# Keys, queries and convolution states turned by VectorE's 32x32 blocks, gates one block later, the ending's mean and root per 128 tokens

## The chip, the cores and the metric

The kernel runs on one core of one Trainium2 chip. The metric is the device time of one execution in microseconds (us). A core has TensorE (PE, matmuls), VectorE (DVE), ScalarE (ACT), GpSimd (Pool) and a queue engine (SP), each with a program of its own that it goes through in order; they wait for each other through semaphores.

## The reference

One layer of a decoder is computed for 256 new tokens (prompt) and 8 running sequences of 4 tokens (sample), 288 tokens in all, with a model width of 2048, all in float32. Cut to its core:

```python
proj = x @ w_in
gB, gC, h, q, k, v, z, b_logit, a_logit, m_a, m_b = split(proj)
conv_out, new_conv_a = causal_depthwise_conv(gC * h, conv_a_buf, conv_a_w)      # width 3
y_a = (gB * conv_out) @ w_a_out
qkv, new_gdn_buf = causal_depthwise_conv(concat([q, k, v]), gdn_buf, gdn_conv_w) # width 4
q, k, v = split(silu(qkv))
qh, kh, vh = l2norm(q), l2norm(k), v                      # 8 heads of 128
beta = sigmoid(b_logit)
g = -exp(a_log) * softplus(a_logit + dt_bias)
o, S = gated_delta_rule(qh, kh, vh, g, beta, S0)          # chunks of 64 tokens
o = o * rsqrt(mean(o * o) + eps) * gdn_norm_w * silu(z)
y_b = o @ w_b_out
merged = sigmoid(m_a) * y_a + sigmoid(m_b) * y_b
x = layer_norm(ALPHA * x + merged @ w_o, ln1)
x = layer_norm(ALPHA * x + square(relu(x @ w_up)) @ w_down, ln2)
```

Outputs are y for prompt and sample, the last rows of both convolutions (2 rows of 1024 and 3 rows of 3072 per sequence), and the delta-rule states S.

## The kernel before

Channels lie on the 128 partitions and the 288 tokens along the free dimension. The weights are read from DRAM once, in 496 blocks of 128 x 4 x 256 values (512 KB). For each block, ACT writes a rounded copy, `hi` (`split_hi`, line 187), and DVE the remainder, `lo` (`split_lo`, recorded at its helper's line 142); PE multiplies the high and low halves of the activations with `hi` (line 217) and the high half with `lo` (line 219), 24 products per block. `raw`, `hi` and `lo` have four buffers each, so the split of block n waits until PE is done with block n-4.

The main loop goes over the blocks. Iteration i issues, in this order: the hi of block i+3, one step of the side work (from block 8 on), the lo of block i+3, the evacuations that are due, the matmuls of block i, and the load of block i+7. What is issued in one iteration runs on each engine in program order; so a product of the side work stands on PE between two blocks, and PE stands still if its operand is late.

Blocks 0 to 23 are the keys, queries and values of the first group of four heads, 24 to 47 those of the second, 48 to 95 the short convolution's, 96 to 111 z; from 112 on follow the output projections and the MLP. The evacuation of a q, k or v group (`conv_evac`) copies into `w`, convolves with three DVE operations, keeps the last rows in `stB` (the other convolution's in `stA`), and an iteration later writes silu into `kq` (keys and queries of a group, channel-major), `kqs` and `vf`.

The side work is a chain of Python generators, a step per block. `gates` (line 941) adds the halves of x into `xf` over four steps, multiplies by the gate weights (line 955), transposes the result `ba`, and computes beta and g; three empty steps follow, then products with constant masks (lines 995 to 1000), exponentials and the copies of gates into the layouts used later (`sx` last). `gdn(G)` (line 1035) is the delta rule for one group. Its first part, which the change rewrites, transposes keys and queries on PE, squares them on ACT, sums the squares on DVE (`red`), and copies the keys to `kdec`:

```python
for c in range(4):
    kt = gtile()
    for hh in range(4):
        pe.transpose(kv[:, hh, :], kq[:, hh, c].rearrange("p s x -> p (s x)"), ident)   # L1072
    act.activation(s2, kv, AF.Square)                                                    # L1074
    for par in range(2):
        act.copy(kdec[rows[par], c], kv[rows[par], par::2, :])                           # L1076
    dve.tensor_reduce(out=red[:, c, :], in_=s2, ...)                                     # L1077
    if c % 2:
        yield
```

Then come the masked gate `gl`, the sums of squares in `ss`, transposes of `kqs`, `kr`, and `glx`: the two halves of `gl`, by ACT (line 1099) and DVE. Two steps later PE multiplies them by a mask (`gr`, line 1107). `gdn(0)` runs from block 20 on, `gdn(1)` after it. `states` (line 1449), after block 96, transposes `stB` and `stA` on PE (line 1462), copies them with ACT (line 1464) and writes them by 24 DMAs from Pool's queue (line 1469).

`final` (line 708) is the ending: from the statistics `mv` (mean and variance, `sd` and `rs` for the root and its inverse) it makes rows `R`, turns them on PE, and adds them as rank-one products (`rank`) to the transposed result (`widen`); `act_unit` scales by ACT and writes out.

Of the kernel before, what the change touches and what calls it, by code (L numbers as in the profile page):

```python
# [9 lines left out]
F32 = mybir.dt.float32  # L10
F32R = mybir.dt.float32r
# [94 lines left out]
def hybrid_kernel(ctx: ExitStack, tc: tile.TileContext, A):  # L106
# [23 lines left out]
    def bc(ap, n):  # L130
        sh = list(ap.shape)
        return ap.unsqueeze(len(sh)).to_broadcast(sh + [n])
# [8 lines left out]
    def tt(out, a, b, op):  # L141
        dve.tensor_tensor(out=out, in0=a, in1=b, op=op)  # L142

    def stt(out, a, s, b, o0, o1):
        dve.scalar_tensor_tensor(out=out, in0=a, scalar=s, in1=b, op0=o0, op1=o1)
# [109 lines left out]
    hmr, bo8 = (cp.tile([P, P], F32R, name=n) for n in ("hmr", "bo8"))  # L255
    stB = cp.tile([P, 24, 27], F32, name="stB")
    stA = cp.tile([P, 8, 18], F32, name="stA")

# [449 lines left out]
    def final(ps):  # L708
# [29 lines left out]
        def out(b, n, c0=0, c1=512):  # L738
            c = slice(512 * n + c0, 512 * n + c1)
            sp.dma_start(A["y_prompt"][0, b * P:(b + 1) * P, c], Y[:, b, c])  # L740

        widen(0, 0)
        widen(1, 0)
        widen(0, 1)
        act.activation(sd, sd, AF.Sqrt, bias=epsc[:, 0:1])
        R4 = R.rearrange("p b (q s) -> p b q s", q=2)
        act.copy(R4[:, :, :, 0:2], bc(mv, 2))
        d = slice(1024, 1536)

        stt(Y[:, 0, d], ph["g2"][:, d], m[:, 0:1], Y[:, 0, d], MUL, SUB)  # L750
        tt(R4[:, :, :, 2], mv, R4[:, :, :, 0], SUB)
        dve.reciprocal(out=rs, in_=sd)
        stt(Y[:, 0, d], Y[:, 0, d], rs[:, 0:1], ph["b0"], MUL, ADD)
        out(0, 2)
        pr = gtile()
        for b in range(2):
            pe.transpose(pr[0:6, b * P:b * P + P], R[:, b, :].bitcast(F32), ident)
        act.copy(ph["st5"], pr[0:6, 0:256])
        stt(r[:, 1:2], m[:, 1:2], -1.0, rs[:, 1:2], MUL, MUL)
        widen(1, 1)  # L760
        rank(wide[0][:, 0], 0, 0)
        act_unit(0, 0, wide[0][:, 0])
# [15 lines left out]
        w12, pq2, w03 = gtile(), gtile(), gtile()  # L778
        widen(1, 2, w12)
        rank(w12, 1, 2)  # L780
        pe.matmul(pq2[:, 0:1], cst("quart"), dv, start=True, stop=True)
        widen(0, 3, w03)
# [38 lines left out]
    warm = tx.tile([P, P], mybir.dt.bfloat16, name="warm")  # L821
    dve.memset(warm, 0.0)
    wps = gtile()

# [3 lines left out]

    warm_up(5)
    xr = [tx.tile([P, 2, 512], F32, name=f"xr{i}") for i in range(4)]  # L830
# [109 lines left out]

    def gates():

# [56 lines left out]
        pe.matmul(q[:, 136:144], cst("lrems"), g[:, 2, :], start=True, stop=True)  # L999
        pe.matmul(q[:, 144:160], cst("lsp"), be[:, 2, :, :], start=True, stop=True)  # L1000
        ge = cp.tile([P, 96], F32, name="gexp")
# [17 lines left out]
        s1 = cp.tile([P, 4, 2], F32, name="s1")  # L1019
        tt(s4, q[:, 128:160].rearrange("p (q h) -> p q h", h=8), bmid(cst("sel"), 4), MUL)  # L1020
        dve.tensor_reduce(out=s1.rearrange("p a b -> p (a b)"), in_=s4.rearrange("p q (g h) -> p (q g) h", h=4),
# [13 lines left out]
    def gdn(G):  # L1035
# [31 lines left out]

        for c in range(4):
            kt = gtile()
            kv = kt.rearrange("p (h c) -> p h c", h=4)  # L1070
            for hh in range(4):
                pe.transpose(kv[:, hh, :], kq[:, hh, c].rearrange("p s x -> p (s x)"), ident)  # L1072
            s2 = sqr[:, 512 * (c % 2):512 * (c % 2) + 512].rearrange("p (h c) -> p h c", h=4)
            act.activation(s2, kv, AF.Square)  # L1074
            for par in range(2):
                act.copy(kdec[rows[par], c], kv[rows[par], par::2, :])  # L1076
            dve.tensor_reduce(out=red[:, c, :], in_=s2, axis=mybir.AxisListType.X, op=ADD)  # L1077
            if c % 2:
# [3 lines left out]
        ssv = ss[:, 0:16].rearrange("p (a c r) -> p a c r", a=2, c=4)  # L1082
        for par in range(2):
            act.copy(ssv[rows[par], 0], red[rows[par], :, par::2])
            act.copy(ssv[rows[par], 1], red[rows[par], :, 1 - par::2])
# [3 lines left out]
        states_in(1)  # L1089
        yield  # L1090
# [3 lines left out]
        act.copy(kr, sp2[:, 0:P])  # L1094
        states_in(2)
        yield
        glf = gl.rearrange("p c r x -> p (c r x)")
        glx = pl.tile([P, 2, 512], F32R, tag="vml", name=nm("glx"))
        act.copy(glx[:, 0], glf)
# [27 lines left out]
        tt(Ef, Ef, bmid(cst("mbias"), 8), ADD)  # L1127
        yield
        act.activation(Ef, Ef, AF.Exp)
        kdf = kdec.rearrange("p c r x -> p (c r) x")  # L1130
# [11 lines left out]
        vt = U128.rearrange("p q x -> p (q x)")  # L1142
        dve.transpose(out=vt, in_=vf.rearrange("p r c a x -> p (r c a x)"))
        vtv = vt.rearrange("p (r c a e) -> p c r a e", r=2, c=4, a=4)
# [24 lines left out]
        yield  # L1169
        move_v(0)  # L1170
        yield
# [276 lines left out]

    def states():
        while cur[0] < mark["z"]:  # L1450
            yield
        tags = ["gl", "vmh", "vml"]
        for src, n, npr, ntl, prompt, sample in (
                (stB, 27, 3, 24, A["new_gdn_conv_prompt"][0, 0], A["new_gdn_conv_sample"][0]),
                (stA, 18, 2, 8, A["new_conv_a_prompt"][0, 0], A["new_conv_a_sample"][0])):
            for q0 in range(0, ntl // 4, 4):
                nq = min(4, ntl // 4 - q0)
                pt = gtile()
                st = gd["pool"].tile([P, 512], F32, tag=tags.pop(), name=nm("st"))
                for q in range(nq):  # L1460
                    t = 4 * (q0 + q)
                    pe.transpose(pt[0:4 * n, q * P:(q + 1) * P], src[:, t:t + 4, :].rearrange("p t r -> p (t r)"),
                                 ident)
                act.copy(st[0:4 * n, 0:nq * P], pt[0:4 * n, 0:nq * P])
                for u in range(4):
                    so = st[n * u:n * u + n, 0:nq * P].rearrange("r (q c) -> r q c", c=P)
                    for dst, r in ((prompt, slice(0, npr)), (sample.rearrange("b j c -> (b j) c"), slice(npr, n))):
                        d = dst.rearrange("r (q u c) -> r q u c", u=4, c=P)
                        gps.dma_start(d[:, q0:q0 + nq, u, :], so[r])
# [64 lines left out]
    for i in range(len(blocks)):  # L1534
# [12 lines left out]
        if i == 7:  # L1547
            tx_cm.__exit__(None, None, None)
            gcm = tc.tile_pool(name="gdn", bufs=1)
            gpool = gcm.__enter__()  # L1550
            gd["pool"] = gpool
            gd["w1"] = [gpool.tile([P, 640], F32, tag=f"w1{u}", name=f"w1{u}") for u in range(2)]
            for w in gd["w1"]:
                gps.memset(w[:, 0:3], 0.0)
            for G in range(2):
# [83 lines left out]
```

## Time and profile before

| | us |
|---|---|
| three runs, median (lowest to highest) | 1668.58 (1668.04 to 1668.66) |
| the profiled execution, its own time | 1668.52 |
| its span | 1666.7 |

| engine | busy us | share of the span | instructions |
|---|---|---|---|
| PE | 1658.0 | 99% | 13169 |
| DVE | 969.2 | 58% | 1289 |
| ACT | 788.8 | 47% | 1231 |
| Pool | 80.0 | 5% | 175 |

The granted clock was 0.998. A line of the waits has the waiting engine and line, the releaser, then the microseconds in total, how often, and the longest. A line of the chain has its start and its length in microseconds. A line of the timeline has start and length, and in square brackets how long the engine was idle before it and what released it. A line of a group gives the number of instructions, then the busy time and the mean in ns, then the idle time ahead of them.

### The profile page before, as it was taken

The page shows a single profiled execution, that of the slowest core. Times are in us where ns is not written, and L with a number is a line of the kernel's source. Part 1 is how long each engine was busy: PE and PEld are TensorE (multiplying, and loading weights), DVE is VectorE, ACT ScalarE, POOL GpSimd, SP SyncE. Part 2 cuts the span into 40 slices and gives each one's busy share as a digit, 9 for nine tenths or more (in the row PEclk, how much of TensorE's full clock was granted, in tenths as well). Part 3 has the DMA queues.
Part 4 walks back from the last instruction along what each step waited for, and adds up shares of the span by engine and source line. Part 5 has one row for each costly group of instructions (what it writes and reads, how often), then busy time and mean ns, then how long its engine had stood idle before and what let it go on. Part 6 is the DMA issues. An engine that isn't in the chain of part 4 may idle for free.

```text
span 1666.7 us, 31341 instructions
## 1 busy us (share of the span) xinstructions
PE 1658.0 (99%) x13169; PEld 1642.8 (99%) x13169; DVE 969.2 (58%) x1289; ACT 788.8 (47%) x1231; POOL 80.0 (5%) x175
## 2 busy tenths in 40 slices
PE   9999999999999999999999999999999999999998
PEld 8999999999999999999999999999999999999998
DVE  6787677667544444457776666444444444444466
ACT  6786757458533333334444455443334433344343
POOL 0100220022200000000000000000000000000000
PEclk9999999999999999999999999999999999999999
DMA  8565466545655555555565555555555555555552
GB/s 271 157 185 166 128 199 186 154 127 171 207 167 166 167 157 174 164 165 165 157 209 164 167 166 163 167 165 165 165 164 165 165 165 167 165 165 167 168 163 89
DMA packets 275347, 279.35 MB, mean 168 GB/s; under 512 B 13779, under 2 KB 269332, under 8 KB 275200
## 3 DMA queue, kind: packets, MB, share of 16 engines
q1 hardware_dynamic: 271334, 266.33, 51.0%
q0 software_dynamic: 3728, 10.96, 2.4%
q8 instruction: 103, 1.69, 0.4%
q14 instruction: 38, 0.31, 0.1%
q10 hardware_dynamic: 144, 0.07, 0.0%
HBM read 269.83 MB, written 7.48 MB: 166 GB/s over the span
## 4 chain that ended last, share of the span: by engine, by line
PE 99%; DVE 1%; DMA 0%; ACT 0%; SPq 0%; issue 0%; DVEq 0%
PE acc L217 63%; PE acc L219 32%; PE g L1209 0%; PE g L1376 0%; PE g L1396 0%; PE g L1399 0%; DMA raw<-in_w_in_dram 0%; PE g L1200 0%; PE g L1138 0%; DVE xf L142 0%; PE g L1354 0%; DVE lo L142 0%; PE g L1388 0%; PE g L1072 0%; PE g L897 0%; PE acc L728 0%
## 5 line engine op out<-in xcount | busy, mean ns | idle before, releaser
L142 DVE TENSOR_TENSOR lo<-raw,hi 128x1024 fp32r<-128x1024 f32 (+1 forms) x503 | 606.0, 1209 | 582.0 <-ACT hi L187 580.9
L187 ACT CAST hi<-raw 128x1024 fp32r<-128x1024 f32 (+1 forms) x499 | 518.9, 1043 | 737.1 <-PE acc L217 648.8
L217 PE MATMUL acc<-xh,hi 128*128 128x288 f32 x1408 | 399.4, 299 | 0.7 <-ACT hi L1491 0.4
L217 PE MATMUL acc<-xl,hi 128*128 128x288 f32 x1408 | 394.3, 295 | 0.0
L219 PE MATMUL acc<-xh,lo 128*128 128x288 f32 x1408 | 301.9, 295 | 0.0
L217 PE MATMUL acc<-dl,hi 128*128 128x288 f32 (+1 forms) x1024 | 287.7, 295 | 0.0
L217 PE MATMUL acc<-dh,hi 128*128 128x288 f32 (+1 forms) x1024 | 287.6, 295 | 0.0
L217 PE MATMUL acc<-hl,hi 128*128 128x288 f32 x1024 | 287.2, 295 | 0.0
L217 PE MATMUL acc<-hh,hi 128*128 128x288 f32 x1024 | 287.1, 294 | 0.0
L217 PEld LDWEIGHTS acc<-xh,hi 128*128 128x128 f32 x1408 | 264.6, 188 | 3.7 <-issue 1.4
L217 PEld LDWEIGHTS acc<-xl,hi 128*128 128x128 f32 x1408 | 264.5, 188 | 1.0
L219 PEld LDWEIGHTS acc<-xh,lo 128*128 128x128 f32 x1408 | 225.9, 188 | 0.2 <-DVE lo L142 0.2
L219 PE MATMUL acc<-hh,lo 128*128 128x288 f32 x1024 | 222.6, 296 | 0.0
L219 PE MATMUL acc<-dh,lo 128*128 128x288 f32 (+1 forms) x1024 | 219.8, 296 | 0.0
L217 PEld LDWEIGHTS acc<-dh,hi 128*128 128x128 f32 x1024 | 193.3, 189 | 0.1
L217 PEld LDWEIGHTS acc<-dl,hi 128*128 128x128 f32 x1024 | 192.8, 188 | 0.1
L217 PEld LDWEIGHTS acc<-hh,hi 128*128 128x128 f32 x1024 | 192.4, 188 | 0.0
L217 PEld LDWEIGHTS acc<-hl,hi 128*128 128x128 f32 x1024 | 192.1, 188 | 0.0
L219 PEld LDWEIGHTS acc<-hh,lo 128*128 128x128 f32 x1024 | 165.0, 188 | 0.0
L219 PEld LDWEIGHTS acc<-dh,lo 128*128 128x128 f32 x1024 | 164.6, 188 | 0.0
L217 PE MATMUL acc<-mh,hi 128*128 128x288 f32 x256 | 72.1, 296 | 0.0
L217 PE MATMUL acc<-ml,hi 128*128 128x288 f32 x256 | 72.0, 295 | 0.0
(401 smaller groups left out, 1395.3 us busy)
## 6 DMA issues: line engine op xcount, KB each, us to landing
raw<-in_w_in_dram SPq DMA_DIRECT2D x175, 512.0 KB, 3.5
raw<-in_w_up_dram SPq DMA_DIRECT2D x128, 512.0 KB, 3.6
raw<-in_w_down_dram SPq DMA_DIRECT2D x128, 512.0 KB, 3.6
raw<-in_w_o_dram SPq DMA_DIRECT2D x32, 512.0 KB, 3.6
raw<-in_w_a_out_dram SPq DMA_DIRECT2D x16, 512.0 KB, 3.6
raw<-in_w_b_out_dram SPq DMA_DIRECT2D x16, 512.0 KB, 3.6
S<-in_state_gdn_dram POOLq DMA_DIRECT2D x8, 512.0 KB, 6.9
out_dram<-S POOLq DMA_DIRECT2D x8, 512.0 KB, 4.5
```

The source lines that it names most:

```text
L142: dve.tensor_tensor(out=out, in0=a, in1=b, op=op)
L187: act.copy(his[i][:, k:k + step], raw[i][:, k:k + step])
L217: pe.matmul(o, h[:, k, c], x, start=st and x is xh_, stop=False)
L219: pe.matmul(o, l[:, k, c], xh_, start=False, stop=en)
```

## The change

- **Start.** Of five bf16 products that run before the data is there, one goes and two float32r ones of 128x128 come. The first slice of x is loaded in smaller parts (`x_first`), with `w_first(1)` ahead of the second half.
- **Gates.** An empty step stands between the sums `xf` and the gate product, so that the steps behind it come a block later. The sample's beta is no longer multiplied by a mask on PE but copied by Pool (`gsb`). The first two steps of `gdn(0)` run inside the gates' empty steps; its other steps follow two blocks earlier than before.
- **gdn.** Keys and queries are turned by DVE in 32x32 blocks, 128x512 in one instruction, into a part of `S0` that isn't loaded yet. ACT squares from there; DVE sums 32 values at a time into `part`; sixteen small Pool copies gather `part` in `red4`, and a DVE reduce makes `red`. The keys go to `kdec` with four copies of 32x256 for each quarter, two quarters on Pool and two on ACT (`move_k`). `glx` is written in the step before `gr`. Two of the four state loads come later.
- **States.** `stB` and `stA` lie in one tile `stBA` padded to 32 columns; DVE turns 128x256 at a time, and 16 Pool DMAs write 128-byte rows. The larger state is written at the end of the first group, the smaller at block 96.
- **Ending.** Root, rows and turning are done for each 128 tokens; the output of one unit is scaled and written in two halves, and a subtraction moves to Pool.

The diff, cut to its core:

```diff
-    warm_up(5)
+    warm_up(4)
+    for _ in range(2):
+        pe.matmul(wps[:, 0:P], warm_r, warm_r, start=True, stop=True)
...
-    x_first(128, 512)
+    x_first(128, 256)
     w_first(1)
+    x_first(256, 512)
...
-    def gates():
+    def gates(first):
...
             tt(xf[0][:, ks] if u < 3 else xf[1], xh[:, ks, 0:NT], xl[:, ks, 0:NT], ADD)
             yield
+        yield
         gb = gtile()
...
-        for _ in range(3):
-            yield
+        sb = cp.tile([P, 2, 8], F32, name="gsb")
+        for w4 in range(4):
+            gps.tensor_copy(sb[32 * w4:32 * w4 + 32], be[96:128, 2])
+        yield
+        next(first)
+        yield
+        next(first)
+        yield
         q = gtile()
...
-        pe.matmul(q[:, 144:160], cst("lsp"), be[:, 2, :, :], start=True, stop=True)
...
         states_in(0)
+        states_in(1)
...
-        for c in range(4):
...
+        kt = S0[:, 2:4].rearrange("p h b e -> p (h b e)").rearrange("p (h n) -> p h n", h=4)
+        part = T([P, 4, 16], "part")
+        for hh in range(4):
+            dve.transpose(out=kt[:, hh], in_=kq[:, hh].rearrange("p c s x -> p (c s x)"))
+            s2 = sqr[:, 512 * (hh % 2):512 * (hh % 2) + 512]
+            act.activation(s2, kt[:, hh], AF.Square)
+            dve.tensor_reduce(out=part[:, hh], in_=s2.rearrange("p (n e) -> p n e", e=32),
+                              axis=mybir.AxisListType.X, op=ADD)
+            if hh < 3:
+                yield
...
+        def move_k(copy, w):
+            d, a, b = places[w]
+            for i in range(4):
+                r = slice(32 * i, 32 * i + 32)
+                copy(kdec[d, :, :, r], ktv[r, a, a, b])
+
+        for d, a, b in places:
+            for i in range(4):
+                gps.tensor_copy(red4[d, i], ptv[32 * i:32 * i + 32, a, b])
         tt(gl, bc(G_["g"][:, :, pr], 64), ...)
...
         act.copy(kr, sp2[:, 0:P])
-        states_in(2)
-        yield
+        move_k(gps.tensor_copy, 0)
+        move_k(act.copy, 1)
+        gps.memset(aT, 0.0)
+        yield
+        dve.tensor_reduce(out=red, in_=red4.rearrange("p i c h -> p c h i"), axis=mybir.AxisListType.X, op=ADD)
+        for par in range(2):
+            act.copy(ssv[rows[par], 0], red[rows[par], :, par::2])
+            act.copy(ssv[rows[par], 1], red[rows[par], :, 1 - par::2])
...
         act.copy(glx[:, 0], glf)
         tt(glx[:, 1], glf, glx[:, 0], SUB)
-        states_in(3)
-        yield
-        gps.memset(aT, 0.0)
-        yield
+        move_k(gps.tensor_copy, 2)
+        yield
+        move_k(act.copy, 3)
         gr = gtile()
...
+    def states_out(t0, t1, npr, n, tag, prompt, sample):
+        st = gd["pool"].tile([P, t1 - t0, 32], F32, tag=tag, name=nm("st"))
+        for t in range(t0, t1, 8):
+            dve.transpose(out=st[:, t - t0:t - t0 + 8]..., in_=stBA[:, t:t + 8]...)
+        for i in range(4):
+            for dst, r0, r1 in ((prompt, 0, npr), (sample..., npr, n)):
+                gps.dma_start(dst.rearrange("r (t i c) -> i r t c", i=4, c=32)[i], st[32 * i + r0:32 * i + r1])
...
     def side():
-        yield from gates()
+        first = gdn(0)
+        yield from gates(first)
         for G in range(2):
             while cur[0] < mark["kqv", G] + 20 or aux:
                 yield
-            yield from gdn(G)
-        aux.append(states())
+            yield from first if G == 0 else gdn(G)
+            if G == 0:
+                states_out(0, 24, 3, 27, "kdec", ...)
+        aux.append(states_a())
```

More of the change, by code (lines that the diff above doesn't have):

```diff
@@ L255, in hybrid_kernel @@
     hmr, bo8 = (cp.tile([P, P], F32R, name=n) for n in ("hmr", "bo8"))
-    stB = cp.tile([P, 24, 27], F32, name="stB")
-    stA = cp.tile([P, 8, 18], F32, name="stA")
+    stBA = cp.tile([P, 32, 32], F32, name="stBA")
+    stB, stA = stBA[:, 0:24, 0:27], stBA[:, 24:32, 0:18]
     gd = {}
@@ L740, in out, with rows, turn_rows @@
             sp.dma_start(A["y_prompt"][0, b * P:(b + 1) * P, c], Y[:, b, c])
+        R4 = R.rearrange("p b (q s) -> p b q s", q=2)
+        pr = gtile()
+        def rows(b):
+            act.activation(sd[:, b:b + 1], sd[:, b:b + 1], AF.Sqrt, bias=epsc[:, 0:1])
+            act.copy(R4[:, b, :, 0:2], bc(mv[:, b], 2))
+            gps.tensor_tensor(out=R4[:, b, :, 2], in0=mv[:, b], in1=R4[:, b, :, 0], op=SUB)
+        def turn_rows(b):
+            pe.transpose(pr[0:6, b * P:b * P + P], R[:, b, :].bitcast(F32), ident)
+            act.copy(ph["st5"][:, b * P:b * P + P], pr[0:6, b * P:b * P + P])
         widen(0, 0)
         widen(1, 0)
+        rows(0)
+        rows(1)
+        turn_rows(0)
         widen(0, 1)
-        act.activation(sd, sd, AF.Sqrt, bias=epsc[:, 0:1])
-        R4 = R.rearrange("p b (q s) -> p b q s", q=2)
-        act.copy(R4[:, :, :, 0:2], bc(mv, 2))
+        turn_rows(1)
         d = slice(1024, 1536)
+        dve.reciprocal(out=rs[:, 0:1], in_=sd[:, 0:1])
         stt(Y[:, 0, d], ph["g2"][:, d], m[:, 0:1], Y[:, 0, d], MUL, SUB)
[L751 to L758, printed above, removed]
+        for c0 in (0, 256):
+            e = slice(1024 + c0, 1280 + c0)
+            stt(Y[:, 0, e], Y[:, 0, e], rs[:, 0:1], ph["b0"][:, c0:c0 + 256], MUL, ADD)
+            out(0, 2, c0, c0 + 256)
+        dve.reciprocal(out=rs[:, 1:2], in_=sd[:, 1:2])
+        rank(wide[0][:, 0], 0, 0)
+        widen(1, 1)
         stt(r[:, 1:2], m[:, 1:2], -1.0, rs[:, 1:2], MUL, MUL)
-        widen(1, 1)
-        rank(wide[0][:, 0], 0, 0)
         act_unit(0, 0, wide[0][:, 0])
@@ L779, in final @@
         widen(1, 2, w12)
+        pe.matmul(pq2[:, 0:1], cst("quart"), dv, start=True, stop=True)
         rank(w12, 1, 2)
-        pe.matmul(pq2[:, 0:1], cst("quart"), dv, start=True, stop=True)
         widen(0, 3, w03)
@@ L822, in hybrid_kernel @@
     dve.memset(warm, 0.0)
+    warm_r = tx.tile([P, P], F32R, name="warm_r")
+    dve.tensor_copy(warm_r, warm)
     wps = gtile()
@@ L1066, in gdn @@
         rows = (slice(0, 64), slice(64, 128))
-        for c in range(4):
[L1069 to L1078, printed above, removed]
-                yield
+        kt = S0[:, 2:4].rearrange("p h b e -> p (h b e)").rearrange("p (h n) -> p h n", h=4)
[7 more added lines that the diff above has]
+            if hh < 3:
+                yield
+        ktv = kt.rearrange("p (r a) (c s b e) -> p a s b c r e", a=2, c=4, s=2, b=2)
+        red4 = T([P, 4, 4, 4], "red4")
+        ptv = part.rearrange("p h (c s b) -> p s b c h", c=4, s=2)
+        places = [(slice(64 * a + 32 * b, 64 * a + 32 * b + 32), a, b) for a in range(2) for b in range(2)]
+        def move_k(copy, w):
[6 more added lines that the diff above has]
+                gps.tensor_copy(red4[d, i], ptv[32 * i:32 * i + 32, a, b])
         tt(gl, bc(G_["g"][:, :, pr], 64),
            cst("lc").unsqueeze(1).unsqueeze(1).to_broadcast([P, 4, 2, 64]), MUL)
[L1082 to L1085, printed above, removed]
         sp2 = gtile()
@@ L1128, in gdn @@
         yield
+        states_in(2)
+        states_in(3)
         act.activation(Ef, Ef, AF.Exp)
@@ L1142, in gdn @@
         vt = U128.rearrange("p q x -> p (q x)")
-        dve.transpose(out=vt, in_=vf.rearrange("p r c a x -> p (r c a x)"))
         vtv = vt.rearrange("p (r c a e) -> p c r a e", r=2, c=4, a=4)
@@ L1169, in gdn @@
         yield
+        dve.transpose(out=vt, in_=vf.rearrange("p r c a x -> p (r c a x)"))
         move_v(0)
@@ L1446, in gdn, with states_a @@
         yield
-    def states():
+    def states_out(t0, t1, npr, n, tag, prompt, sample):
+        st = gd["pool"].tile([P, t1 - t0, 32], F32, tag=tag, name=nm("st"))
+        for t in range(t0, t1, 8):
+            dve.transpose(out=st[:, t - t0:t - t0 + 8].rearrange("p t c -> p (t c)"),
+                          in_=stBA[:, t:t + 8].rearrange("p t c -> p (t c)"))
+        for i in range(4):
+            for dst, r0, r1 in ((prompt, 0, npr), (sample.rearrange("b j c -> (b j) c"), npr, n)):
+                gps.dma_start(dst.rearrange("r (t i c) -> i r t c", i=4, c=32)[i], st[32 * i + r0:32 * i + r1])
+    def states_a():
         while cur[0] < mark["z"]:
             yield
[L1452 to L1469, printed above, removed]
-                yield
+        states_out(24, 32, 2, 18, "gl", A["new_conv_a_prompt"][0, 0], A["new_conv_a_sample"][0])
+        yield
     def side():
-        yield from gates()
+        first = gdn(0)
+        yield from gates(first)
         for G in range(2):
@@ L1476, in side @@
                 yield
-            yield from gdn(G)
-        aux.append(states())
+            yield from first if G == 0 else gdn(G)
+            if G == 0:
+                states_out(0, 24, 3, 27, "kdec", A["new_gdn_conv_prompt"][0, 0], A["new_gdn_conv_sample"][0])
+        aux.append(states_a())
     cur = [0]
@@ L1554, in hybrid_kernel @@
                 gps.memset(w[:, 0:3], 0.0)
+            gps.memset(stBA, 0.0)
             for G in range(2):
```

5 lines of the change are left out of this document (3 added, 2 removed).

## The prediction

> **What bounds the kernel now.** I read the page first: busy shares, slices, and the chain that ended last.
>
> ```profile
> PE 1658.0 (99%) x13169; PEld 1642.8 (99%) x13169; DVE 969.2 (58%) x1289; ACT 788.8 (47%) x1231; POOL 80.0 (5%) x175
> DVE  6787677667544444457776666444444444444466
> ACT  6786757458533333334444455443334433344343
> PE 99%; DVE 1%; DMA 0%; ACT 0%; SPq 0%; issue 0%; DVEq 0%
> ```
>
> TensorE (PE) is the path nearly everywhere, so work taken off PE is time, and work added to VectorE (DVE), ScalarE (ACT) or GpSimd (Pool) is free only while PE never waits for it. The averages of 58% and 47% hide that both are at 6 to 8 tenths in the first eleven slices, where the side work runs. Next come the waits of PE, and the chain at three places.
>
> ```profile
> PE g L955 <- DVE xf L142: 1.1, 1, 1.1
> PE g L687 <- ACT r L682: 0.2, 1, 0.2
> PE g L649 <- DVE acc L142: 0.4, 1, 0.4
> ...
> 2.69 4.89 DMA raw<-in_w_in_dram
> 7.60 0.41 ACT hi L1491
> ...
> 54.35 0.53 PE acc L217 x4
> 54.88 0.27 PE acc L219 x2
> ```
>
> PE waits for hardly anything: the gate product waits 1.1 us for the sums xf. Six products take 0.80 us, so a block of 24 takes 3.2 us; that is the period in which ACT and DVE must do a block's split and whatever else is put there.
>
> **What comes off PE.**
>
> ```profile
> L1072 PE MATMUL g<-cf,kq 128*128 128x128 f32 x32 | 4.1, 272 | 0.0
> L1462 PE MATMUL g<-cf,stB 128*108 128x128 f32 x6 | 1.0, 272 | 0.0
> 80.72 0.87 PE g L1072 x8
> 74.02 0.23 PE g L1000 x2
> GB/s 271 157 185 166 128 199 186 154 127 171 207 167 166 167 157 174 164 165 165 157 209 164 167 166 163 167 165 165 165 164 165 165 165 167 165 165 167 168 163 89
> ```
>
> The durations (272 ns) overlap; the chain's piece tells the cost on the path, 0.87/8 = 0.109 us each. The 32 key and query transposes make 3.48 us, the eight state transposes (six of stB, two of stA of the same kind) 0.87. The gate product for sample beta, L1000, goes: 0.23. [...]
>
> The gate sums get a block more: the 1.1 us go. Next late would be the transposes of ba, also a block later. At the start w_first(1) is issued ahead of half of x: 256 KB at the first slice's 271 GB/s is 0.97 us, the most it can gain; block 1 then waits for load(1), which has the same bytes ahead and one more issue: between 0 and 1.0, I take 0.6. The other warm-up products run before the first data. At the end PE has the same products in another order; only the two waits of 0.4 and 0.2 above can go: I take 0.2. Loss there is excluded neither, but no wait is added that isn't on DVE or ACT work moved earlier.
>
> Sum of gains: 3.48 + 0.87 + 0.23 + 1.1 + 0.6 + 0.2 = 6.5 us.
>
> **What it puts in the place of it, group 0.** The first group's side work starts two blocks earlier, inside the gates' steps. In iteration i, ACT does hi(i+3), then the side step, then the due evacuations; DVE does the side step, lo(i+3), evacuations. hi(n) can't start before PE has done block n-4, whose buffer it takes. PE meets the product gr at the head of block 24, and in program order it stands still until glx is there. Before, glx was written two steps (6.4 us) ahead of gr; now one step. The rows that price the steps:
>
> ```profile
> 63.22 1.05 ACT L187 CAST hi<-raw 128x1024 fp32r<-128x1024 f32 x1 [1.58 <-PE acc L217]
> 64.29 1.28 ACT L972 ACT_TABLE_LOAD   x1
> 68.88 1.04 ACT L187 CAST hi<-raw 128x1024 fp32r<-128x1024 f32 x1
> 69.82 0.36 ACT L275 COPY w<-acc 128x256 f32<-128x256 f32 x1
> 70.99 1.05 ACT L187 CAST hi<-raw 128x1024 fp32r<-128x1024 f32 x1
> 74.16 1.28 ACT L1003 ACT_TABLE_LOAD   x1
> 76.98 0.21 ACT L1024 ACTIVATE sx<-s 128x4 f32<-128x4 f32 x1 [0.90 <-DVE s L1021]
> 77.20 1.28 ACT L294 ACT_TABLE_LOAD   x1
> 79.37 2.18 ACT L187 CAST hi<-raw 128x1024 fp32r<-128x1024 f32 x2
> ...
> L1074 ACT ACTIVATE vmh<-g 128x512 f32<-128x512 f32 x8 | 4.8, 597 | 0.1
> L1148 ACT COPY v<-U 32x256 f32<-32x256 f32 x32 | 12.9, 404 | 0.4
> L1099 ACT CAST glx<-gl 128x512 fp32r<-128x512 f32 x2 | 1.2, 618 | 0.0
> ...
> L142 DVE TENSOR_TENSOR lo<-raw,hi 128x1024 fp32r<-128x1024 f32 x493 | 601.8, 1224 | 581.5 <-ACT hi L187 580.9
> L145 DVE SCALAR_TENSOR_TENSOR w<-w,hw 128x312 f32<-128x312 f32 x72 | 39.3, 547 | 5.9 <-ACT w L279 4.2
> L645 DVE STREAM_TRANSPOSE Y<-acc 128x256 f32<-128x256 f32 x12 | 4.8, 424 | 0.0
> L1143 DVE STREAM_TRANSPOSE U<-vf 128x1024 f32<-128x1024 f32 x2 | 2.5, 1239 | 0.0
> L1077 DVE TENSOR_REDUCE red<-vmh 128x4 f32<-128x512 f32 x8 | 5.5, 685 | 3.4 <-ACT vmh L1074 3.4
> ```
>
> Instructions overlap a little, so I take start to start: hi 0.94 (68.88 to 69.82); a projection's evacuation 1.17 (69.82 to 70.99); hi with the gates' three table loads 5.66 (63.22 to 68.88); table load and four silus 2.17 (77.20 to 79.37). The 128x512 transpose isn't in the trace: between 0.42 and 1.24, I take 0.69, midway by elements.
>
> ACT's list from hi(19), which can't start before PE ends block 15 (time 0), to glx, us:
> - hi(19), the gates' loads, evacuation: 5.66 + 1.17 = 6.83
> - hi(20), Square, evacuation: 0.94 + 0.57 + 1.17 = 2.68
> - hi(21), Square, silus: 0.94 + 0.57 + 2.17 = 3.68
> - hi(22), the second gates' step, without its wait: 0.94 + 2.26 = 3.2 (the step is 74.16 to 77.20 less 0.90, partly overlapped)
> - hi(23) and hi(24), each with a Square and an evacuation: 5.36
> - hi(25), two small Squares and kr (0.8), four copies of 32x256 (some 1.6 by L1148), silus: about 5.6
> - hi(26), four small copies (0.6), glx 0.62: 2.2
>
> That is 29.6, and DVE's second half of glx, 0.69, makes 30.3. PE needs for its eight blocks and the side products between them 25.6 + 1.0 + 0.2 = 26.8. So gr is 3.5 us late even if ACT never waits: this is the lower bound.
>
> But ACT waits. Each Square now reads what DVE transposed, and DVE reaches that transpose only behind lo and the evacuation of the step before, which waits for ACT's own. Walking both queues: DVE finishes the gate arithmetic at 6.6, lo(19) at 7.8, evacuation 9.4, first transpose 10.1, while ACT was done with hi(20) at 7.8: idle 2.3. The second transpose ends at 14.9, idle 2.0. lo(22) stands behind the sx operations, which wait for an Exp behind a table load (21.0), and ends at 22.2 where PE wants it at 20.9: PE stands 1.3. The third and fourth transposes cost ACT 1.0 and 2.0. Together 7.3 us, so glx is complete at about 38, 11.2 after 26.8. Afterwards PE has three blocks of splits in hand, so that the delay is kept and not enlarged. Bounds 3.5 and 13 (a transpose at 1.24 adds 4 x 0.55, less what then hides); I take 11.2, since every idle piece follows from the program's order.
>
> **Group 1.** The same steps without gates. Eight copies of 32x256 in each of two steps at the first group's end (they are there before too) leave ACT 3.6 us behind PE, the three state transposes (3 x 0.43) and the first key transpose now stand in one DVE step, and the loop transpose, Square, reduce, lo (0.69 + 0.6 + 0.69 + 1.13 = 3.1) has no room against 3.2 to recover. I get glx at 21.8 from the head of block 64, where gr comes at 19.4: 2.4 late; bounds 0 (its normal lead hides it) and 4.
>
> **States and Pool.** Of 24 DMAs 16 remain, with 128-byte rows: 27 x 24 x 4 = 2592 rows instead of 648 for the larger state. The small ones were off the path.
>
> ```profile
> L1469 POOL DMA_DIRECT2D out_dram<-st x24 | 13.3, 564 | 2.8 <-ACT st L1464 2.3 <-issue 0.5
> DMA to landing us min/median/max: 3.4/4.4/6.0
> L1294 POOL CAST kr<-hl x32: 283/290/1272, 174.9 to 347.5; 32x128 fp32r<-32x128 f32 x32
> L1294 POOL CAST kr<-hl 32x128 fp32r<-32x128 f32 x32 | 15.1, 471 | 28.8 <-ACT hl L1285 26.7 <-DVE hl L142 0.7
> ```
>
> Eight issues are 4.5 us, and the first write over their source (kdec, by Pool and ACT) comes three steps, 9.6 us, later. At up to 6.0 to land that is 10.5 for the last: covered within a us; I take 0. If landing grew with the rows, ACT would wait some 10 us; no row bears that out, and it stays in the upper end.
>
> **Sum.** 1668.52 (the profiled execution, 0.06 under the median) - 6.5 + 11.2 + 2.4 = 1675.6; I say 1675.5. Differences within 0.2%, 3.3 us, I count as no change.
>
> **Rivals.**
> 1. ACT's queue alone decides: the ping-pong is hidden by work that I placed too strictly, and group 1 is covered. Then -6.5 + 3.5: 1665.5. For it: none of PE's waits quoted above is for a split, so there was room. Against: ACT's 0.90 us for DVE at sx, and DVE's 3.4 for the Squares, show that the two do wait for each other already. Chance 0.18.
> 2. No new wait at all: 1662.0. It needs ACT's list 3.5 us shorter than its rows. 0.10.
> 3. Slower still, by Pool. The squares' sums now go through 16 small Pool copies, then a DVE reduce, ACT copies, and only then glx. The casts of L1294 take 0.28 alone and up to 1.27, mean 0.47: some stand for the length of one lo. From the last partial sum at 29.3 to the copies of ACT at 36.3 are 7 us; it decides when a copy takes over 0.44 on average. At 0.7 it adds 4 us in group 0: 1679.5. [...] 0.20.
> 4. My forecast, 1675.5, with 1672 to 1679 as its own range. 0.52.
>
> **Numbers.** The range 1664 to 1682 holds the forecast, rival 3 and the upper half of rival 1, and leaves out rival 2, some of rival 1 and a late landing. Faster: rival 2 and half of 1, 0.19. Same: half of 1 and the forecast's low edge, 0.13. Slower: 0.68.
>
> **What would show it.** In the profile after: a PE wait for glx at gr of several us between 95 and 110 us, with ACT idle before each Square for DVE's transposes; a smaller one between 265 and 285; no wait for xf; none of the transposes on PE. I am wrong if PE's waits stay under 4 us in all, or if the long one names Pool or a DMA.

## The result and the profile after

The changed kernel takes 1686.64 us (median of 4 runs, 1685.92 to 1687.25) against 1668.62 before in the same measurement: ratio 1.0107, 95% interval 1.009 to 1.0125. It is slower by 18 us; forecast was slower by 7. The profiled execution took 1686.86, its span is 1685.1.

The page of after: the engines' busy time, three rows of the slices, and the chain.

```profile
PE 1661.8 (99%) x13128; PEld 1644.6 (98%) x13128; DVE 977.6 (58%) x1306; ACT 788.8 (47%) x1230; POOL 103.8 (6%) x222
PE   9979998999999999999999999999999999999998
DVE  5778777757544444546776666454444444445465
PEclk9989999999999999999999999999999999999998
PE 93%; ACT 2%; DVE 2%; DMA 1%; POOL 1%; issue 1%; SPq 0%; POOLq 0%; ACTq 0%; DVEq 0%
```

DVE and ACT have hardly more work than before (977.6 against 969.2, 788.8 against 788.8). But PE has two dents, in the third slice (group 0) and the seventh (group 1), and the granted clock falls in the third. PE is now 93% of the chain, not 99%. The waits of PE in after:

```profile
PE g L1145 <- ACT glx L1138: 14.0, 2, 9.1
PE acc L219 <- DVE lo L142: 1.0, 2, 0.8
PE g L840 <- DVE warm L833: 1.0, 1, 1.0
PE acc L217 <- ACT hi L187: 0.7, 1, 0.7
PE g L1121 <- ACT kqs L296: 0.5, 1, 0.5
PE g L751 <- POOL R L748: 0.4, 1, 0.4
PE g L649 <- DVE acc L142: 0.4, 1, 0.4
PE g L687 <- ACT r L682: 0.2, 1, 0.2
```

Line 1145 is gr. It waits twice, once per group: 9.1 us in group 0 and 4.9 in group 1. The wait for xf (1.1) is gone. The wait for `warm` (1.0, at the start) and the last two were there before, too. ACT's timeline in group 0 shows why glx is late: before each of the four Squares it stood idle for VectorE's transpose.

```profile
76.06 0.63 ACT L1097 ACTIVATE vmh<-S 128x512 f32<-128x512 f32 x1 [2.31 <-DVE S L1095]
80.81 0.63 ACT L1097 ACTIVATE vmh<-S 128x512 f32<-128x512 f32 x1 [2.00 <-DVE S L1095]
89.19 0.63 ACT L1097 ACTIVATE vmh<-S 128x512 f32<-128x512 f32 x1 [1.12 <-DVE S L1095]
93.94 0.63 ACT L1097 ACTIVATE vmh<-S 128x512 f32<-128x512 f32 x1 [2.00 <-DVE S L1095]
```

The prediction had 2.3, 2.0, 1.0 and 2.0. The chain of after around gr (pieces left out between the first and the last of Pool's sixteen copies, around VectorE's reduce, and among the products behind):

```profile
94.60 0.70 DVE part L1098
95.35 0.59 POOL red L1116
95.98 1.10 POOL red L1116
...
102.02 0.21 POOL red L1116
102.25 0.27 DVE red L1132
...
103.17 0.63 ACT glx L1138
103.84 1.52 PE g L1145 x2
105.36 0.96 PE acc L217 x4
...
109.49 0.53 PE acc L217 x4
```

Pool's copies carry the chain from 95.35 to 102.2. ACT's own queue, with hi(26), ended at 102.35, so both arrived together. Behind the wait four products take 0.96 us, and 0.53 again only from 109.49 on. PE's windows of after say the same: a window, PE's busy time (and products), the granted clock, the DMA share, GB/s.

```profile
94.40:103.80 9.40, 0.29 (x3) 0.74 0.43 128
104.60:109.40 4.80, 4.80 (x21) 0.53 0.49 120
110.00:114.00 4.00, 4.00 (x37) 1.00 0.97 293
```

To see where time goes, here is how late PE reaches the first product with lo in some blocks, in us against the trace of before (worked out from the records of both; negative is earlier; blocks 13 to 64 hold group 0, 64 to 112 group 1 and the state transposes that PE no longer does):

| block | after | e2 | e4 | e10 | e11 | e13 | e14 |
|---|---|---|---|---|---|---|---|
| 8 | 0.8 | 0.1 | 0.4 | 0.6 | 0.3 | 2.5 | 0.5 |
| 13 | -0.5 | -1.2 | -0.9 | -0.6 | -0.9 | 1.3 | -0.8 |
| 24 | 10.3 | 9.0 | -2.8 | 4.8 | 1.8 | -0.7 | -1.0 |
| 33 | 11.7 | 9.1 | 8.8 | 5.3 | 3.3 | 10.6 | -1.0 |
| 39 | 14.6 | 15.0 | 8.9 | 8.8 | 6.4 | 11.0 | -1.0 |
| 64 | 12.0 | 12.3 | 8.9 | 6.1 | 3.8 | 10.2 | -1.0 |
| 74 | 17.3 | 16.1 | 17.0 | 6.8 | 2.6 | 8.4 | -1.0 |
| 112 | 16.4 | 15.2 | 16.2 | 6.8 | 3.0 | 10.0 | -1.0 |
| 495 | 16.5 | 15.2 | 16.2 | 6.9 | 3.0 | 10.1 | -0.9 |

So after is 0.8 late from the start, wins 1.3 by the gates (blocks 8 to 13), loses 12.5 in group 0 and 4.4 in group 1, and the ending, from there to the spans' difference of 18.4, loses the remaining 1.9.

### The profile page after: what moved, and what is told of

It reads as the page before. It is cut to its first block, busy times and chain, and to the rows that moved or that the text cites. A ratio compares the mean times of both kernels' runs of the same rounds, so it can differ in the third digit from the quotient of the medians.

```text
span 1685.1 us, 31333 instructions
## 1 busy us (share of the span) xinstructions
PE 1661.8 (99%) x13128; PEld 1644.6 (98%) x13128; DVE 977.6 (58%) x1306; ACT 788.8 (47%) x1230; POOL 103.8 (6%) x222
## 4 chain that ended last, share of the span: by engine, by line
PE 93%; ACT 2%; DVE 2%; DMA 1%; POOL 1%; issue 1%; SPq 0%; POOLq 0%; ACTq 0%; DVEq 0%
PE acc L217 60%; PE acc L219 30%; POOL red L1116 1%; DVE lo L142 1%; ACT hi L187 1%; DMA xs<-in_x_sample_dram 1%; DMA xr<-in_x_prompt_dram 0%; DVE w L145 0%; PE g L1416 0%; ACT ao L1479 0%; PE g L1436 0%; PE g L1439 0%; ACT vmh L1097 0%; DVE S L1095 0%; PE g L1249 0%
```

## The experiments

Each is the changed kernel with the edit shown, unless it says otherwise. Behind each median stands in brackets how far it is from that of the kernel before in the same measurement; for the changed kernel this is +18.0. Its ratio has the interval 1.009 to 1.0125. Of the edits to the changed kernel, only e5 lies above that interval with its own and only e10, e11 and e13 below; for the others the times alone don't tell, and the waits and the table carry the reading.

**e1: glx ahead of the sums in its step.**

```diff
+        act.copy(glx[:, 0], glf)
+        tt(glx[:, 1], glf, glx[:, 0], SUB)
         dve.tensor_reduce(out=red, in_=red4..., ...)
         for par in range(2):
             act.copy(ssv[rows[par], 0], ...)
-        act.copy(glx[:, 0], glf)
-        tt(glx[:, 1], glf, glx[:, 0], SUB)
```

> The changed kernel, but within the same step glx (ACT copy and VectorE subtraction) stands ahead of the reduce of red4 and the four small copies that wait for it. In the changed kernel Pool's last copy of red4 ended at 102.0 us and ACT's own queue was ready at 102.35 in group 0, and at 280.8 against 279.45 in group 1. Theory 1 (Pool's chain and ACT's queue are both late, Pool more so in group 1): PE's wait at gr falls from 9.1 to some 8 in group 0 and from 4.9 to some 2.5 in group 1, 3 us and a little clock less: about 1683. Rival (the wait is ACT's queue alone, Pool only happens to end near it): 0.8 less in each group, 1685. Rival (Pool alone): both waits shrink by the 7 us of Pool's copies, to 2 and 0, about 1673.

1684.76 us (+15.1). The wait at gr fell to 8.2 in group 0 and to 2.5 in group 1 (10.7 in all): theory 1. Pool's sums cost 2.4 of group 1's 4.9, with the copies that stand behind them; in group 0 the wait is 0.9 shorter, and ACT's four small copies alone take 0.6 of that.

**e2: PE kept busy while it waits.**

```diff
+        for _ in range(64 - 32 * G):
+            pe.matmul(gr[:, 0:NT], xh[:, 0, 0:P], xh[:, 0, 0:NT], start=True, stop=True)
         for u in range(2):
             pe.matmul(gr, hmr, glx[:, u], ...)
```

> The changed kernel with products of no use ahead of gr, 64 in group 0 and 32 in group 1, of 0.1325 us each: 8.5 and 4.2 us, within the waits of 9.4 and 5.2, so that glx still comes last. The output is the same. Theory (after the long wait PE runs at half clock, which costs 2.6 us in group 0 and 2.1 in group 1): the granted clock stays at 1.0 behind both and the time falls by 4 to 5 us, to 1682. Rival (the slow products behind the wait are something else, or the half clock costs nothing because ACT and VectorE are behind anyway): no change within 1 us, 1686.6.

1685.25 us (+15.6): 1.4 less than the changed kernel, or 2.4 less against before, and not 4 to 5. PE's windows of e2, during and behind group 0's wait:

```profile
94.00:103.00 9.00, 8.44 (x65) 1.00 0.40 120
104.00:109.00 5.00, 5.00 (x37) 1.00 0.45 136
```

The clock stayed up, and 37 products went through in 5 us where after had 21 in 4.8. At block 33 it is 2.6 us ahead of after (9.1 against 11.7); 0.7 of that it had at block 13 already, so the clock is worth 1.9. But at block 39 nothing is left of it (15.0 against 14.6): PE then waits for xt, a later step of the group on ACT, and behind that wait the clock falls all the same. Its row in the waits, and the windows during and behind it:

```profile
PE g L1251 <- ACT xt L1284: 2.0, 1, 2.0
```

```profile
149.40:151.40 2.00, 0.02 (x1) 1.00 0.92 267
151.70:155.00 3.30, 3.30 (x94) 0.50 0.79 248
```

So the half clock is real, and in group 0 it costs nothing net, because the chain of ACT and VectorE sets when xt is there. That is the rival's second reason. In group 1 keeping the clock up is worth 1.5 us (2.9 late from block 64 to 112, where after has 4.4).

**e3: glx two steps earlier.** The old lines of gl and glx go; pieces are left out.

```diff
         for hh in range(4):
+            if hh == 3:
+                tt(gl, ...)
+                act.copy(glx[:, 0], glf)
             dve.transpose(out=kt[:, hh], ...)
+            if hh == 3:
+                tt(glx[:, 1], glf, glx[:, 0], SUB)
```

> The changed kernel, but gl and glx are made at the fourth key transpose, two steps ahead of gr, while ACT waits for VectorE anyway; nothing of them waits for red4. Theory (the two long waits are those of glx behind the squares' sums): PE's waits at gr fall below 1 us in group 0 and to 0 in group 1, the clock stays up, and 9 + 4.9 + 4.7 us come back, less 2 to 3 for a split of a later block that now stands behind the reduce: about 1670 to 1672. Rival (PE is held by the splits themselves, glx only shows it): the waits move to hi and lo with the same sum, 1682 to 1686.

1684.05 us (+14.4): the rival. At gr PE waits 0.2 us at most, and it waits for splits and later steps instead. The waits of PE in e3:

```profile
PE acc L219 <- DVE lo L142: 9.1, 5, 3.6
PE g L1264 <- ACT mx L1255: 2.0, 1, 2.0
PE g L1251 <- ACT xt L1284: 0.9, 1, 0.9
```

glx only shows that ACT and VectorE are late as a whole; what isn't waited for at gr is waited for at lo.

**e4: group 0 from block 20, not inside the gates.**

```diff
         yield
-        next(first)
         yield
-        next(first)
         yield
         q = gtile()
```

> The changed kernel with the two steps of group 0 taken out of the gates' empty steps, so that group 0 runs from block 20 as before the change. Theory 1 (as predicted: the lateness of group 0 comes from sharing the gates' steps with their table loads): the wait at gr in group 0 falls from 9.1 to about 2, and with the clock that is 10 us: 1677. Rival (each group's own chain of transposes, Squares, Pool copies and the one step to gr is late, as in group 1, which has no gates): the wait falls only to about 5 to 7, 1682 to 1684.

1686.47 us (+16.8). The wait in group 0 is 8.1 (at block 26), in group 1 7.7. The rival was right that each group is late by itself, and even it had put the wait too low. By the table group 0 loses 9.8 us (12.5 in after) and group 1 7.3 (4.4 in after). With the gates' table loads out of the way, ACT stands 5.1 us at the Squares of group 0, and then 2.3 for the sums that come through Pool, for which it had hardly waited in after. The first of its small copies, in e4 and in after:

```profile
105.76 0.20 ACT L1132 COPY ss<-red 64x8 f32<-64x8 f32 x1 [2.28 <-DVE red L1130]
102.54 0.20 ACT L1134 COPY ss<-red 64x8 f32<-64x8 f32 x1 [0.19 <-DVE red L1132]
```

So the wait does not need the table loads; why group 1 loses more in e4, with the same code, isn't shown.

**e5: the sixteen small copies on ACT.**

```diff
-                gps.tensor_copy(red4[d, i], ptv[32 * i:32 * i + 32, a, b])
+                act.copy(red4[d, i], ptv[32 * i:32 * i + 32, a, b])
```

> The changed kernel with the sixteen small copies of red4 on ACT instead of Pool. In the changed kernel they take 6.9 us on Pool in group 0 and 6.1 in group 1, three to six of them 0.5 to 1.1 us long where VectorE's lo runs beside them, the others 0.2 and 0.24 from start to start. On ACT a small copy follows the one before it after 0.1 to 0.2 us: 2.5 us for sixteen. Theory (Pool's chain is late by itself): in group 1 the wait at gr falls from 4.9 to 1.5 or less, in group 0, where ACT's own list is as late as Pool, it falls by 0 to 2; what is won in group 0 is lost again at the later wait for xt, so 1681 to 1683 in all. Rival (ACT is the bound in both groups): the waits grow by 2.5 each, 1690.

1692.51 us (+23.4); the waits are 13.6 and 6.9. A copy followed the one before it after 0.23 us, so sixteen are 3.6 on ACT, and the waits grew by 4.5 and 2.0: the rival, which had 2.5 in each group. What is added to ACT's list delays gr, more so in group 0.

**e6: the kernel before, with only the ending.** The edit is the part called Ending in the section on the change.

> The kernel before with only the ending of the change. In the traces the stretch from the last product of the last block to the end of the last scaling was 8.9 us before and 11.1 after. Theory (the ending costs by itself: PE waits for Pool's subtraction, 0.4, and its clock falls to half 2 to 3 us earlier): 2.2 us slower, 1671.9. Rival (the ending is slow only behind what came earlier): 0, 1669.7. As predicted: 0.2 faster.

1670.3 against 1669.1, ratio 1.0006 (0.9997 to 1.0015): the times don't tell. In the traces, its span is 2.5 longer than before's, 1.8 of that are there at block 495 (it waited 1.5 for x at the start), which leaves 0.7 for the ending. One wait of PE in e6 is new against before, and is 0.4 of it:

```profile
PE g L751 <- POOL R L748: 0.4, 1, 0.4
```

The other traces settle it. In all eleven that have the new ending, the stretch from block 495 to the end is 0.7 to 2.0 us longer than in before; in the four that keep the old one (e7, e8, e13, e14) it is the same within 0.1. So the new ending costs at least 0.7. In after it lost 1.9: there the clock was at half from 1676 on (0.50), 9.2 us before the end, in before 6.1 and in e6 6.1; four of line 732's products have a mean of 544 ns in after and 470 in e6. Of the five traces that lose over 1.5, four have the clock fall that early; e2 loses 1.6 without it, and why isn't shown.

**e7 and e14: the kernel before, with gates one block later and states by VectorE's blocks.** The larger state goes through the buffer U128 at the end of group 0. Both runs are of the same kernel.

> The kernel before with two parts of the change: the gates one block later (with the sample's beta by Pool), and the convolution states by VectorE's blocks, the larger one written at the end of group 0 from the buffer of U128. Key transposes, start and ending as before. Theory (these two parts are worth what PE no longer does, 1.1 + 0.23 + 0.87): 2.2 us faster than before, ratio 0.9987. Rival (VectorE, busy for 15.5 of 15.9 us in blocks 28 to 33, gives the block back as a wait for lo near block 33): 0 to 1 us faster.

> The kernel with only the gates a block later and the states by VectorE's blocks, once more, since its first interval (ratio 0.9987 to 1.0005) doesn't tell 2 us from nothing. In the traces PE reached the last block 1.9 us earlier than before the change. Theory: ratio 0.9988, 2 us faster. Rival: what the start's transfers vary by, some 2 us from run to run, covers it: 0.9996.

1668.4 against 1669.1 (0.9996, 0.9987 to 1.0005), and 1667.9 against 1669.19 (0.9994, 0.9985 to 1.0003). Both are a little faster, by 0.7 and 1.3 us, and neither interval leaves out no difference. In the traces PE is 1.9 and 0.9 earlier at block 495; e14 had lost 0.5 at the start, where e7 had won 0.5. Both win 1.2 to 1.3 by the gates and 0.9 by the states between blocks 104 and 112, and both lose 0.9 between blocks 74 and 85, where PE waits for xt, as it doesn't in before:

```profile
PE g L1213 <- ACT xt L1246: 0.6, 1, 0.6
```

So what is left is about the gain of the gates, whose product for the sample's beta is 0.2 of it. Why xt comes later there isn't shown.

**e8: start and ending of before, group 0 later, glx early, sums on ACT.** The edits of e3, e4 and e5 together, and the two old parts.

> The changed kernel with start and ending of before, group 0 from block 20 on, gl and glx at the fourth key transpose, and the sums' copies on ACT. Theory (what costs in a group is the chain through Pool and the late glx; VectorE and ACT have room for the transposes once these are gone): all waits in the two groups under 3 us, with 4.35 + 1.3 off PE: 1666 to 1668. Rival (VectorE has no room in blocks 28 to 33, so each group gives back 2.5 us of transposes and the round trips of the Squares): waits for lo of 5 to 8 us, 1671 to 1675.

1688.14 us (+19.0), worse than either bound: waits of 10.3 for lo, 2.4 for hi and 2.2 for ACT's evacuation. It mixes several edits, so it doesn't say which of them costs; that ACT has no room for the sixteen copies is e5's result.

**e9: sums left out.** A memset stands for fifteen of the sixteen copies, so the sums are wrong.

```diff
-        for d, a, b in places:
-            for i in range(4):
-                gps.tensor_copy(red4[d, i], ptv[32 * i:32 * i + 32, a, b])
+        gps.memset(red4, 1.0)
+        gps.tensor_copy(red4[0:32, 0], ptv[0:32, 0, 0])
```

> The changed kernel with one of the sixteen small Pool copies left and a memset for the other fifteen, so that the sums of squares are left out and red waits for one copy only. If ACT's list is what is late, as forecast: in group 0 ACT still comes to the small copies at 102.4 us and the wait at gr shrinks by 0.2 only, in group 1, where ACT had stood 1.6 us for red, by 1.6 to 2; 1683 to 1685. If Pool's copies are what is late: by 5 to 6 in each group, 1674.

1684.5 us (+15.0).

**e10: Squares of what isn't turned.** All instructions stay, but ACT needn't wait for VectorE's transpose, and the sums are of other values.

```diff
-            act.activation(s2, kt[:, hh], AF.Square)
+            act.activation(s2, kq[:, hh].rearrange("p c s x -> p (c s x)"), AF.Square)
```

> The changed kernel with the Squares taken of the keys and queries before they are turned, so that ACT needn't wait for VectorE's transpose (the sums are then of other values; all instructions stay). As forecast, ACT stands 7.3 us for these transposes in group 0: without that its list ends 7 us earlier, but Pool's sixteen copies (6.9 us, after the fourth part) then come last, and the wait at gr in group 0 falls from 9.1 to about 6. If the round trip costs nothing: no change, 1686.

1676.11 us (+6.6).

**e11: both edits.**

> The changed kernel with both: Squares of what isn't turned, and the sixteen copies replaced by one and a memset. Forecast: what is left is ACT's list by itself, the lower bound of the prediction: a wait of 3.5 us at gr in group 0, 0 to 1 in group 1. With the clock not falling, and with little given back at the later wait for xt, 1673 to 1677. Rival (VectorE's own work is the bound): the same time comes back as waits for lo, 1682.

1672.52 us (+3.0). These three divide the wait at gr. Its row in the waits of PE, first e9:

```profile
PE g L1144 <- ACT glx L1137: 12.2, 2, 8.9
```

then e10:

```profile
PE g L1145 <- ACT glx L1138: 7.2, 2, 5.5
```

and e11:

```profile
PE g L1144 <- ACT glx L1137: 3.5, 1, 3.5
```

| | group 0 | group 1 | over before |
|---|---|---|---|
| changed kernel | 9.1 | 4.9 | 18.0 |
| e9, no sums | 8.9 | 3.3 | 15.0 |
| e10, no round trip | 5.5 | 1.7 | 6.6 |
| e11, neither | 3.5 | 0 | 3.0 |

Taking Pool's copies away is worth some 3 us (within the spread of the times; PE is 2.1 nearer at block 112), taking the wait for the transposes away 11.4, both 15. What e9 wins lies in group 1, where ACT stood for the sums in after:

```profile
281.08 0.20 ACT L1134 COPY ss<-red 64x8 f32<-64x8 f32 x1 [1.62 <-DVE red L1132]
```

With neither, 3.5 us are left in group 0, the prediction's lower bound. Part of that match is chance: the bound counts to VectorE's half of glx, 0.7 later, while the wait ends with ACT's half; and ACT still waits 0.95 for VectorE in that list.

**e12: glx early and no sums.** e3 and e9 together.

> The kernel with gl and glx made early, and the sixteen copies replaced by one and a memset. With glx early alone PE's waits had moved to lo, 2.8 and 3.9 us in group 0 and 1.9 in group 1, behind the reduce that waits for Pool. If Pool's copies hold VectorE there, these waits go, and 5 to 8 us come back: 1676 to 1679. If VectorE is short of room anyway: 1682 to 1684.

1682.47 us (+13.0), 1.4 nearer to before than e3: the waits for lo stay, 8.5 us. VectorE isn't held by Pool there.

**e13: the same work in another order.** With start and ending of before, and nothing left out of the work. Beside the order of turning, squaring and summing, glx is made earlier, and gr comes one block later than in the change. In short:

```diff
-        for hh in range(4):
-            dve.transpose(kt[:, hh]); Square(kt[:, hh]); sums(hh)
-            if hh < 3:
-                yield
+        turn(0); yield
+        square(0); turn(1); yield
+        square(1); sums(0); turn(2); yield
+        square(2); sums(1); turn(3); gl; glx[0]; yield
+        square(3); sums(2); glx[1]; sums(3)
```

> The changed kernel with start and ending of before and the same work in another order: each key transpose is issued one step ahead of its Square and each sum one step behind it, gl and glx are made at the fourth transpose, and gr comes one block later than in the change (one block earlier than before). Nothing is left out. Theory (the round trip ACT to VectorE of the four Squares is the main cost): ACT no longer waits at the Squares, PE's wait at gr is under 1 us in both groups, and what is left is a few us at the later wait for xt and lo, where VectorE has no room: 1669 to 1673. Rival (VectorE's added 2.8 us per group, and not the order, bound the kernel): waits for lo and xt of 8 us and more, 1676 and up.

1676.69 us (+7.5, ratio 1.0047, 1.0035 to 1.006), between theory and rival: 10.5 nearer to before than the changed kernel, of which the old ending may have some 2. At the Squares ACT waits 0.5 us in all, and PE not at gr; but in group 0 ACT stands 3.0 for gl ahead of glx, and 1.2 for the sums. By the table, group 1 is even, with what PE no longer does there counted in (10.2 at block 64, 10.0 at 112), and group 0 still loses 8.9 (1.3 to 10.2). The waits of PE in e13, and the chain that leads to one of them:

```profile
PE acc L219 <- DVE lo L142: 6.8, 4, 2.5
```

```profile
115.50 1.13 DVE lo L142
116.64 0.61 DVE gl L142
117.27 0.69 DVE E L142
117.96 0.33 DVE gl L142
118.31 0.43 DVE gl L142
118.75 0.42 DVE gl L142
```

VectorE goes from one instruction to the next there. All four waits for lo lie in blocks 28 to 32, and between blocks 28 and 33 VectorE was busy for 15.5 of 15.9 us in before already: it has no room there to make up what came late.

## Why the prediction was wrong

The sign was right, the time not: 1675.5 with a range to 1682, and 1686.64 came. The signs that it named came too: the long wait at gr, ACT idle before each Square, a smaller wait in group 1, none for xf. Against the forecast, the spans' 18.4 hold 1.4 more at the start, 3.3 in group 0, 4.6 in group 1, 2.1 at the ending, and 0.2 less by the gates. By its own terms:

- **Group 0, the wait at gr.** Forecast: glx 38 us after PE ended block 15, 11.2 late, by ACT's list of 30.3 and 7.3 of waits. That step held: ACT's four waits came as forecast (7.4 in all), glx was whole at 104.5, 38.5 after block 15's end at 66.0. PE reached gr 28.7 after that end, not 26.8, as it stood 0.5 for kqs and 0.8 for a lo on the way; so the wait at gr was 9.1. (30.3 and 7.3 make 37.6, which the prediction rounds to 38.) That ACT waits for VectorE's transposes is the main cause: e10 and e11 show it by taking the wait away.
- **Group 0, what comes after.** "The delay is kept and not enlarged" failed. Net of the 1.74 and 0.23 us that PE no longer does, 11.2 would be 9.2 between blocks 13 and 64; it was 12.5. The 3.3 more are half clock behind the wait, or else the wait for xt that takes its place when the clock stays up (e2, which loses 13.5 there): the term that was missing is that what follows has its own pace on ACT and VectorE.
- **Group 1**, forecast 2.4 late, bounds 0 to 4. The wait was 4.9, outside. This is the largest miss: net of what PE no longer does the forecast was -0.2 from block 64 to 112, and 4.4 came. The step that was mis-sized left out Pool: its copies hold ACT 1.6 us there (e9: 3.3). The round trips count there as well: e10 leaves 1.7. The half clock behind the wait adds 1.5 (e2: 2.9 against 4.4). The rest of the excess has no run of its own.
- **Ending**, forecast 0.2 faster, was 1.9 slower. "No wait is added" failed: the subtraction that went to Pool is waited for (0.4), and the two waits of 0.4 and 0.2 that were to go both stayed. The new ending costs 0.7 in e6; in after the clock fell 3 us sooner besides.
- **Start**, forecast 0.6 faster. In this trace 0.8 slower at block 8; but the same code gave 0.1 in e2 and 0.2 in e12, and the old start 1.8 in e6, 0.5 in e14 and -0.5 in e7. What the start varies by from run to run hides any effect.
- **Gates and states**: 1.3 forecast 1.1 in blocks 8 to 13; the states' 0.87 came too, cleanest in e14: from 0.1 earlier at block 104 to 1.0 at 112; but e7 and e14 lose as much again between blocks 74 and 85. Key transposes off PE: 3.48 were forecast, and no run takes them off by themselves; even e11, with no round trip and no sums, is 3.0 slower than before.
- **Rival 3**, Pool as the last to arrive with 1679.5: Pool's copies took 6.9 us where 7 was the point from which they decide, and they did not in group 0 (e9: 0.2), though barely; they mattered in group 1. The 0.7 us a copy that its 1679.5 is added up from is shown by no run: the sixteen of group 0 took 0.43 on average. The copies in both groups took 194 to 1109 ns, and the four of 1.1 us all ran beside a lo and ended within 0.06 us of its end.
- The half clock was in no term. The clock was 0.53 behind after's 9.1 us of waiting, and the two stretches at half clock ahead of the ending lasted 10.24 and 6.83 us in after. A shorter wait was enough as well: it was 0.50 behind e2's wait of 2.0 us, and 0.62 behind e1's waits of 2.5 and 0.2 in group 1; e10's of 1.7 and 0.2 there left 1.00. What sets the clock beyond that isn't shown.

What stays open: what exactly in group 0's later steps sets the arrival of xt, and so how the 3.3 us divide. That no change of order could hide them was not shown. e13 changes several things at once, and gr a block later was not run by itself. The fastest version that ran is the one of e7 and e14, and its gain, about 1 us, isn't clear of the spread.

## What to carry to other kernels

When work moves from the bound engine to two others that pass data back and forth within one step, don't price it by busy time: walk both queues in program order, since the handovers cost the queue in front of them 7.4 us of waits here, for 2.8 us of transposes. Issue the producer a step ahead of the consumer: e13, which did that, made glx earlier and put gr a block later, brought some 8 of 18 us back without the ending; which part of it did how much isn't shown. And where two engines have no room for some blocks, a mended wait can come back as another, as it did in e3 (14.0 us at gr in after, at most 0.2 in e3, but 9.1 for lo), so look for the stretch with the least slack first.

## What the runs showed of the hardware

PE's granted clock fell to half behind a wait as short as 2.0 us (e2, 0.50 from 151.7 to 155.0), and in after it came back 5.3 and 4.3 us after the ends of the two waits of 9.1 and 4.9. It stayed at 1.00 behind e10's waits of 1.7 and 0.2 us in group 1.

A small copy of 32x16 on Pool took 0.2 us in after, and up to 1.1 while VectorE's lo ran beside it; the same copies on ACT followed each other after 0.23 us in e5. Sixteen took 6.9 and 6.1 us on Pool and 3.6 on ACT, but there they lengthened the queue that was already late. A transpose of 128x512 took 0.70 us on VectorE, as interpolated.
